# Seven products of sums of quarters (Strassen) for the second matrix of layer 0's MLP, in two of its eight chunks

## The chip, the core and the metric

The kernel runs on one core of a Trainium2 chip. The metric is the device time of one execution in microseconds (us); 2351.22 us is the median of 3 runs of the kernel before. Names of engines: PE is TensorE's matmul, PEld its weight load, DVE is VectorE, ACT is ScalarE, POOL is GpSimd, SP is SyncE, which issues the DMAs here.

## The reference, cut to what matters

The kernel computes two blocks of a network in float32. The second block has two layers over two streams of 256 tokens each, x and a context; each layer mixes tokens, normalises, and runs an MLP. The change touches the MLP of the second block's layer 0 alone, which both streams go through:

```python
def sq_relu_mlp(u, w1, b1, w2, b2):
    return jnp.square(jax.nn.relu(u @ w1 + b1)) @ w2 + b2

# in layer l, D_MODEL = 1024, hidden width 4096:
x = layer_norm(alpha * x + g2 * sq_relu_mlp(x * (1.0 + sc2) + sh2, w1[l], b1[l], w2[l], b2[l]), ln2_g[l], ln2_b[l])
if with_ctx:   # layer 0
    ctx = layer_norm(alpha * ctx + cg2 * sq_relu_mlp(ctx * (1.0 + csc2) + csh2, w1[l], ...), ln2_g[l], ln2_b[l])
```

## The kernel before, in words

**Precision.** PE multiplies in a format of fewer bits than float32, so every operand is split into a high part (an ACT cast) and a low part (a DVE subtraction of the high part from the original), and each product is three matmuls: high by high, high by low, low by high (`mm3`, L350 to L352). A weight tile of 128x1024 goes through `w()`: SP loads the raw tile `wr`, ACT casts it to `wh` (L343), DVE makes `wl` (L344). Raw, high and low tiles have four buffers each.

**The MLP of layer 0** (about 1415 to 1768 us of the trace) works on 512 tokens, four token tiles of 128: tiles 0 and 1 are the context, 2 and 3 are x. The 4096 hidden features are taken in eight chunks of 512, counted hc = 0 to 7. `up(hc)` multiplies four weight tiles of `w1` (eight k-tiles of 128 each) with the input `uh`, `ul`, which gives a chunk of hidden features; ACT makes relu and square and the high part `hh` (L431), DVE the low part `hl` (L432). `down(hc)` multiplies that chunk with four weight tiles of `w2`, for each half nn of the 1024 output features and each half kc of the chunk's features, over four token tiles: 96 matmuls of 512 columns. Results land in PSUM (tiles `mm`, six banks) and are added onto the accumulators `facc` in SBUF by DVE (L1677; chunk 0 is copied by ACT, L1675). In the loop up(hc+1) stands ahead of down(hc), so a pair of 96 + 96 matmuls repeats seven times; down(7) is left at the end.

**Side work.** Each `w()` ends with one step of a generator of other work. In chunks 1 to 4 this is the modulation of layer 1: `mr` tiles are loaded and multiplied onto `macd` by DVE (L892), four steps of 128x512 per loaded tile. After it come the residual rows. Each engine executes its instructions in one fixed order, in which the side work is interleaved.

**The end.** In chunks 6 and 7 `tail` multiplies the results by a gate row (`tl`, L1707) and adds them to the residual `resb` (L1710). In down(7) the token tiles 2 and 3 come first, then 0 and 1. When tiles 2 and 3 are done, their statistics run (BN_STATS L1037, BN_AGGR L1038, `brs`, `bmr` L1048), their scaling on DVE (L1054) and ACT (L1052), and then PE transposes them (L1015, tiles `tp`) into the input of layer 1. The transposes stand in PE's order behind 84 of down(7)'s 96 matmuls, and layer 1's first matmuls behind them. Layer 1's own MLP goes through the same function `mlp`.

## Time and profile before

| what | value |
|---|---|
| median of 3 runs | 2351.22 us (2349.1 to 2352.89) |
| the profiled execution's own time | 2352.55 us |
| its span | 2350.8 us |
| PE, PEld busy | 2278.8 us, 1967.8 us |
| DVE, ACT, POOL busy | 1712.0 us, 1117.2 us, 68.9 us |
| mean granted clock of TensorE | 0.989 |

All rows come from one profiled execution. The span is the time between its first and its last instruction. A busy time counts how long an engine had an instruction in work; instructions overlap in an engine's pipeline, so the distance between two starts can be shorter than the duration shown. Idle time on an engine that is not the bottleneck costs nothing by itself. The clock is in parts of full speed, 1.00 being 2.4 GHz and 0.50 being 1.2 GHz.

### The profile page before, as it was taken

How to read it: one execution, taken by the hardware profiler on the slowest of the kernel's cores; microseconds unless marked ns; L12 is line 12 of the kernel's file. 1: busy time of each engine (PE TensorE's matmuls, PEld its weight loads, DVE VectorE, ACT ScalarE, POOL GpSimd, SP SyncE). 2: the span in 40 equal slices, each digit the busy share in tenths (PEclk: the TensorE clock that was granted, in tenths of full speed). 3: DMA queues.
4: the chain of work that ended last, by engine and by line, in shares of the span. 5: the costliest groups of instructions: out<-in, count | busy, mean ns of one | idle time of the engine just before them, and what ended most of it. 6: DMA issues, size and time to landing. Idle time of an engine off the chain costs nothing.

```text
span 2350.8 us, 35308 instructions
## 1 busy us (share of the span) xinstructions
PE 2278.8 (97%) x13784; PEld 1967.8 (84%) x13796; DVE 1712.0 (73%) x2779; ACT 1117.2 (48%) x1702; POOL 68.9 (3%) x72
## 2 busy tenths in 40 slices
PE   8999989999999999999999999999999999998997
PEld 7989868889999888778777778888889898787996
DVE  6788878977766668985755777677568778776667
ACT  5655545554465444433453326434226543544653
POOL 1011100000000000000000000000000000000000
PEclk9999999999999999999999999999999999999999
DMA  5666546765555543223213735556324344345663
GB/s 199 217 188 191 186 138 225 256 217 191 187 179 186 187 154 111 68 72 94 94 47 106 238 95 179 168 174 197 120 90 150 118 136 127 97 138 180 203 190 115
DMA packets 124743, 364.73 MB, mean 155 GB/s; under 512 B 31840, under 2 KB 33632, under 8 KB 124576
## 3 DMA queue, kind: packets, MB, share of 16 engines
q1 hardware_dynamic: 124576, 362.47, 48.4%
q8 instruction: 108, 1.77, 0.3%
q14 instruction: 59, 0.48, 0.1%
HBM read 357.02 MB, written 3.31 MB: 153 GB/s over the span
## 4 chain that ended last, share of the span: by engine, by line
PE 52%; DVE 5%; issue 1%; ACT 1%; POOL 0%; DVEq 0%; POOLq 0%
PE mm L350 16%; PE mm L351 16%; PE mm L352 15%; PE mm L1437 1%; DVE cy L1149 1%; PE mm L1451 1%; DVE wl L344 1%; PE tp L718 1%; PE mm L1328 1%; PE tp L901 0%; PE tp L1015 0%; PE mm L1286 0%; DVE bst L1037 0%; DVE tl L1707 0%; DVE resb L1710 0%
## 5 line engine op out<-in xcount | busy, mean ns | idle before, releaser
L343 ACT CAST wh<-wr 128x1024 fp32r<-128x1024 f32 (+1 forms) x544 | 566.5, 1044 | 889.7 <-PE mm L351 475.5
L344 DVE TENSOR_TENSOR wl<-wr,wh 128x1024 fp32r<-128x1024 f32 (+1 forms) x544 | 659.3, 1214 | 333.6 <-ACT wh L343 324.8
L351 PE MATMUL mm<-ul,wh 128*128 128x256 f32 (+1 forms) x2224 | 704.5, 319 | 2.6 <-DVE ul L432 1.3
L352 PE MATMUL mm<-uh,wl 128*128 128x256 f32 (+1 forms) x2224 | 704.3, 319 | 2.7 <-DVE wl L344 2.7
L350 PE MATMUL mm<-uh,wh 128*128 128x256 f32 (+1 forms) x2224 | 699.9, 321 | 4.7 <-ACT m_q L1253 1.5
L350 PEld LDWEIGHTS mm<-uh,wh 128*128 128x128 f32 x2224 | 417.0, 190 | 43.1 <-ACT wh L343 5.0
L352 PEld LDWEIGHTS mm<-uh,wl 128*128 128x128 f32 x2224 | 422.3, 190 | 34.9 <-DVE wl L344 3.7
L351 PEld LDWEIGHTS mm<-ul,wh 128*128 128x128 f32 x2224 | 422.5, 190 | 33.9 <-issue 1.8
L351 PE MATMUL mm<-wl,hh 128*128 128x512 f32 x640 | 249.6, 391 | 0.0
L352 PE MATMUL mm<-wh,hl 128*128 128x512 f32 x640 | 249.2, 391 | 0.0
L350 PE MATMUL mm<-wh,hh 128*128 128x512 f32 x640 | 247.6, 391 | 0.0
L892 DVE SCALAR_TENSOR_TENSOR macd<-mr,silu_c,macd 128x512 f32<-128x512 f32 x336 | 238.3, 745 | 7.2 <-DMA mr<-in_w_mod 5.2
L350 PE MATMUL mm<-wh,uh 128*128 128x256 f32 x576 | 165.4, 291 | 2.7 <-ACT qk L575 1.5
L351 PE MATMUL mm<-wl,uh 128*128 128x256 f32 x576 | 163.5, 286 | 1.4 <-DVE wl L344 1.4
L352 PE MATMUL mm<-wh,ul 128*128 128x256 f32 x576 | 163.0, 285 | 0.1
L350 PEld LDWEIGHTS mm<-wh,hh 128*128 128x128 f32 x640 | 120.0, 188 | 28.1 <-issue 3.4
L352 PEld LDWEIGHTS mm<-wh,hl 128*128 128x128 f32 x640 | 120.1, 188 | 26.6 <-issue 0.8
L351 PEld LDWEIGHTS mm<-wl,hh 128*128 128x128 f32 x640 | 120.1, 188 | 26.5 <-DVE hl L432 0.8
L1149 DVE SCALAR_TENSOR_TENSOR cy<-hpad,vecl,cy 128x512 f32<-128x512 f32 (+1 forms) x240 | 136.8, 611 | 0.0
L350 PEld LDWEIGHTS mm<-wh,uh 128*128 128x128 f32 x576 | 108.5, 190 | 9.7 <-issue 4.6
L351 PEld LDWEIGHTS mm<-wl,uh 128*128 128x128 f32 x576 | 109.2, 190 | 3.4 <-DVE wl L344 2.1
L352 PEld LDWEIGHTS mm<-wh,ul 128*128 128x128 f32 x576 | 109.1, 190 | 0.7 <-DVE ul L465 0.3
(292 smaller groups left out, 2817.4 us busy)
## 6 DMA issues: line engine op xcount, KB each, us to landing
wr<-in_m SPq DMA_DIRECT2D x128, 512.0 KB
wr<-in_w SPq DMA_DIRECT2D x128, 512.0 KB
wr<-in_w_in SPq DMA_DIRECT2D x116, 512.0 KB
mr<-in_w_mod SPq DMA_DIRECT2D x96, 512.0 KB
wr<-in_a_wqkv SPq DMA_DIRECT2D x72, 512.0 KB
wr<-in_b_win SPq DMA_DIRECT2D x24, 512.0 KB
wr<-in_w_out SPq DMA_DIRECT2D x16, 512.0 KB
wr<-in_w_uq SPq DMA_DIRECT2D x16, 384.0 KB
```

Of the source, the lines that this page charges most:

```text
L343: self.last_hi = nc.scalar.copy(hi[:, :n], raw[:, :n]).ins
L344: self.last_lo = nc.vector.tensor_tensor(lo[:, :n], raw[:, :n], hi[:, :n].bitcast(F32), ALU.subtract).ins
L350: mm(out, lh, rh, start=first, stop=False)
L351: mm(out, lh, rl, start=False, stop=False)
L352: self.last_mm = mm(out, ll, rh, start=False, stop=last).ins
L718: nc.tensor.transpose(tp[:, b * P:b * P + P], pm[:, b * P:b * P + P], self.ident)
L892: nc.vector.scalar_tensor_tensor(out=a, in0=raw[:, k], scalar=sc, in1=a, op0=ALU.mult, op1=ALU.add)
L1149: nc.vector.scalar_tensor_tensor(out=ys[ft], in0=src, scalar=wk, in1=ys[ft], op0=ALU.mult, op1=ALU.add)
L1328: nc.tensor.matmul(pn[:, d * 130:d * 130 + 129], dts[d][:, s, i * P:i * P + P], v[:, s, 0:129], start=s == ks[0], stop=s == ks[-1])
L1437: nc.tensor.matmul(sc[:, 0:n * P], qs[hp * 2 + i][:, t * P:t * P + P], ks[:, hp * 2 + i, 0:n * P], start=True, stop=True)
L1451: nc.tensor.matmul(pos[hp][i * 64:i * 64 + 64, t * P:t * P + P], v[:, j, h * 64:h * 64 + 64], pt[i][:, j * P:j * P + P], start=j == 0, sto ...
```

## The change

Layer 0's MLP gets a function of its own, `mlp_wide`; layer 1 keeps `mlp`. In the chunks hc = 2 and hc = 4 (`SEVEN`) the product of the hidden chunk and its part of `w2` is taken in quarters: the hidden activations by token half (256 tokens) and feature half kc, the weights by kc and output half nn. Seven products (`PRODUCTS`, Strassen's scheme) take the place of eight. For each: a sum or difference of two activation quarters (`as`, DVE, in five of seven), its split into `ah` (ACT) and `al` (DVE), a sum or difference of two raw weight quarters (`bs`, DVE, 128x1024, in five of seven), its split in the buffers of `wh` and `wl`, 12 matmuls into two PSUM banks, and for each output quarter that it belongs to two adds or subtractions onto `facc` (24 in all per chunk, where there were eight). The steps of up(hc+1) and of the seven products alternate as `TURNS` says.

The other chunks keep their 96 matmuls, but split the hidden activations in four pieces of 128x512 at the start of the down step (`down_plain`, `down_last`), from a ring of four `ah` and four `al` buffers, in place of two pieces of 128x1024 right after up. `tail` for the sum of the first seven chunks is written after the loop (`result`) and no longer within chunk 6. The rows of the residual and the gates take turns in three buffers instead of five.

```diff
+PRODUCTS = (
+    (((0, 0),), None, ((0, 1), (1, 1)), ALU.subtract, ((0, 1, ALU.add), (1, 1, ALU.add))),
+    (((1, 0), (0, 0)), ALU.subtract, ((0, 0), (0, 1)), ALU.add, ((1, 1, ALU.add),)),
...
+    (((0, 1), (1, 1)), ALU.subtract, ((1, 0), (1, 1)), ALU.add, ((0, 0, ALU.add),)),
+)
+SEVEN = (2, 4)
+TURNS = (0, 0, 1, 1, 0, 1, 1, 0, 1, 1, 1)
...
+        def split_a(src):
+            ah = self.t(self.xm, [P, 2, half], "ah", F32R, bufs=4)
+            al = self.t(self.xm, [P, 2, half], "al", F32R, bufs=4)
+            self.split(ah, al, src)
+            return ah, al
+        def down(hc, rs):
...
+            def raw(kc, nn):
+                if (kc, nn) not in Bs:
+                    Bs[kc, nn] = t = self.t(self.xm, [P, 1024], "wq", bufs=3)
+                    self.last_w = nc.sync.dma_start(t, w2[nn, hc * 2 + kc].rearrange("p k f -> p (k f)")).ins
+                    self.spin(self.side_n)
+                return Bs[kc, nn]
+            for i, (qa, opa, qb, opb, outs) in enumerate(PRODUCTS):
+                y = quarter(rs, qa[0])
+                if opa is not None:
+                    y_ = self.t(self.xm, [P, 2, half], "as")
+                    nc.vector.tensor_tensor(y_, y, quarter(rs, qa[1]), opa)
+                    y = y_
+                ah, al = split_a(y)
+                ws = [raw(*q) for q in qb]
+                w = ws[0]
+                if opb is not None:
+                    w = self.t(self.xm, [P, 1024], "bs")
+                    nc.vector.tensor_tensor(w, ws[0], ws[1], opb)
+                bh = self.t(self.wp, [P, 1024], "wh", F32R, bufs=self.wbufs[1])
+                bl = self.t(self.wp, [P, 1024], "wl", F32R, bufs=self.wbufs[1])
+                self.last_hi = nc.scalar.copy(bh, w).ins
+                self.last_lo = nc.vector.tensor_tensor(bl, w, bh.bitcast(F32), ALU.subtract).ins
+                W = WT(bh, bl, 2, 512)
+                pts = [self.ps() for _ in range(nj)]
+                for j in range(nj):
+                    self.lin_t(pts[j], W, 0, 512, ah, al, j * P)
+                for j in range(nj):
+                    for T, nn, op in outs:
+                        a = acc(T * nj + j, nn)
+                        nc.vector.tensor_tensor(a, a, pts[j], op)
...
+        def down_plain(hc, rs):
+            hid = [[split_a(quarter(rs, (T, kc))) for T in range(2)] for kc in range(2)]
...
+        for hc in range(7):
+            u, d = up(hc + 1), down(hc, rs) if hc in SEVEN else None
+            for step in TURNS if d else (0,) * 4:
+                if step:
+                    next(d)
+                else:
+                    rs_ = next(u)
+            if d is None:
+                down_plain(hc, rs)
+            rs = rs_
+        for j in range(4):
+            for nn in range(2):
+                result(j, nn, acc(j, nn))
+        down_last(rs)
...
-            self.mlp(uh, ul, q0, 512, A[f"w1_{l}"], A[f"w2_{l}"], lambda f: self.vecl(f"b1_{l}", f), evac,
-                     self.by_quarters(self.make_u([0], aff, *u)) + [(0, KT, 0, 256)] if l == 0 else self.by_quarters(), MT[2], ready)
+            if l == 0:
+                self.mlp_wide(uh, ul, A["w1_0"], A["w2_0"], bias, accs, result,
+                              self.by_quarters(self.make_u([0], aff, *u)) + [(0, KT, 0, 256)], MT[2], ready)
```

The order of instructions on DVE where chunk 2's products end, in the changed kernel. `facc` rows are adds onto the accumulators, `bs` is a sum of two weights, `al` a low part of activations, `wl` a low part of a weight (`wl_15060` that of the seventh product, `wl_15085` of the next up), `macd` is side work:

```order
L873 TENSOR_TENSOR facc_2397_13767<-facc_2397_13767,mm_14997 128x512 x2
L861 TENSOR_TENSOR bs_15057<-wq_15019,wq_14783 128x1024
L873 TENSOR_TENSOR facc_2398_13768<-facc_2398_13768,mm_14998 128x512 x2
L449 TENSOR_TENSOR al_15250<-r_14687,ah_15249 128x512
L1036 SCALAR_TENSOR_TENSOR macd_14737<-mr_14954,silu_c_85,macd_14737 128x512 x2
L449 TENSOR_TENSOR al_15254<-r_14851,ah_15253 128x512
L873 TENSOR_TENSOR facc_2397_13767<-facc_2397_13767,mm_15033 128x512
L873 TENSOR_TENSOR facc_2399_13769<-facc_2399_13769,mm_15033 128x512
L873 TENSOR_TENSOR facc_2398_13768<-facc_2398_13768,mm_15034 128x512
L873 TENSOR_TENSOR facc_2400_13770<-facc_2400_13770,mm_15034 128x512
L865 TENSOR_TENSOR wl_15060<-bs_15057,wh_15059 128x1024
L361 TENSOR_TENSOR wl_15085<-wr_15082,wh_15084 128x1024
```

The same engine in the kernel before, at the adds that follow chunk 1's down step and the start of the pair with chunk 2, from one low part of a weight to the next ones:

```order
L344 TENSOR_TENSOR wl_15009<-wr_15006,wh_15008 128x1024
L892 SCALAR_TENSOR_TENSOR macd_14725<-mr_15012,silu_c_85,macd_14725 128x512 x2
L1677 TENSOR_TENSOR facc_2397_13767<-mm_14841,facc_2397_13767 128x512
L1677 TENSOR_TENSOR facc_2398_13768<-mm_14842,facc_2398_13768 128x512
L892 SCALAR_TENSOR_TENSOR macd_14725<-mr_15012,silu_c_85,macd_14725 128x512 x2
L1677 TENSOR_TENSOR facc_2399_13769<-mm_14843,facc_2399_13769 128x512
L1677 TENSOR_TENSOR facc_2400_13770<-mm_14844,facc_2400_13770 128x512
L344 TENSOR_TENSOR wl_15045<-wr_15042,wh_15044 128x1024
L1677 TENSOR_TENSOR facc_2397_13767<-mm_14921,facc_2397_13767 128x512
L344 TENSOR_TENSOR wl_15098<-wr_15095,wh_15097 128x1024
```

Between two low parts there stood at most four adds and four steps of side work; now there also stand the sum that the low part is made from, and pieces of activations for the chunk after.

PE at the same place of the changed kernel: `mm_15063` and `mm_15064` belong to the seventh product, `mm_15033` and `mm_15034` to the sixth, `mm_15080`, `mm_15081` and `mm_15167` to the up step that follows:

```order
L368 MATMUL mm_15034<-wl_15030,ah_15015 128x512
L369 MATMUL mm_15034<-wh_15029,al_15016 128x512
L367 MATMUL mm_15063<-wh_15059,ah_15053 128x512
L367 MATMUL mm_15064<-wh_15059,ah_15053 128x512
L367 MATMUL mm_15080<-uh_13388,wh_15084 128x512
L368 MATMUL mm_15080<-ul_13389,wh_15084 128x512
L367 MATMUL mm_15081<-uh_13388,wh_15120 128x512
L368 MATMUL mm_15081<-ul_13389,wh_15120 128x512
L367 MATMUL mm_15167<-uh_13388,wh_15171 128x512
L368 MATMUL mm_15167<-ul_13389,wh_15171 128x512
L368 MATMUL mm_15063<-wl_15060,ah_15053 128x512
L369 MATMUL mm_15063<-wh_15059,al_15054 128x512
```

Eight matmuls that use only high parts stand ahead of the first one that uses `wl_15060`.

DVE at the end of the stage in the changed kernel, up to the statistics (`bmr`) and the scaling of token tile 2 (`resb_2319`); `resb_2317` and `resb_2318` are the tiles of the context:

```order
L361 TENSOR_TENSOR wl_16772<-wr_16769,wh_16771 128x1024
L1182 BN_AGGR bmv_16559<-bst_16561 128x2
L1861 TENSOR_TENSOR resb_2317_13355<-resb_2317_13355,tl_16683 128x512
L1181 BN_STATS bst_16573<-resb_2320_13358 128x6
L1858 TENSOR_TENSOR tl_16686<-mm_16592,row_14241 128x512
L361 TENSOR_TENSOR wl_16785<-wr_16782,wh_16784 128x1024
L423 TENSOR_SCALAR brs_16560<-bmv_16559 128x1
L1181 BN_STATS bst_16697<-resb_2317_13355 128x6
L1182 BN_AGGR bmv_16571<-bst_16573 128x2
L1861 TENSOR_TENSOR resb_2318_13356<-resb_2318_13356,tl_16686 128x512
L1192 TENSOR_SCALAR bmr_16567<-bmv_16559,brs_16560 128x1
L1198 TENSOR_SCALAR resb_2319_13357<-resb_2319_13357,bmv_16559,brs_16560 128x512
```

The same place in the kernel before:

```order
L1710 TENSOR_TENSOR resb_2320_13358<-resb_2320_13358,tl_16364 128x512
L1038 BN_AGGR bmv_16379<-bst_16381 128x2
L1037 BN_STATS bst_16393<-resb_2320_13358 128x6
L406 TENSOR_SCALAR brs_16380<-bmv_16379 128x1
L1038 BN_AGGR bmv_16391<-bst_16393 128x2
L406 TENSOR_SCALAR brs_16392<-bmv_16391 128x1
L1048 TENSOR_SCALAR bmr_16387<-bmv_16379,brs_16380 128x1
L1054 TENSOR_SCALAR resb_2319_13357<-resb_2319_13357,bmv_16379,brs_16380 128x512
L344 TENSOR_TENSOR wl_16571<-wr_16568,wh_16570 128x1024
L1707 TENSOR_TENSOR tl_16495<-mm_16403,row_14237 128x512
L344 TENSOR_TENSOR wl_16584<-wr_16581,wh_16583 128x1024
```

The weights' low parts and the context's tail stood behind `bmr` and the scaling, and stand ahead of them now.

## Rows read from the trace of the kernel before

**Rows 1.** The page's first part: engine, busy us, share of the span, instructions.
```profile
span 2350.8 us, 35308 instructions
PE 2278.8 (97%) x13784; PEld 1967.8 (84%) x13796; DVE 1712.0 (73%) x2779; ACT 1117.2 (48%) x1702; POOL 68.9 (3%) x72
```

**Rows 2.** Busy time by stretch, pairs 2 to 5; columns as the first line.
```profile
core 0: us, PE busy (x) PEld busy (x) DVE busy (x) ACT busy (x) POOL busy (x), PEclk, DMA share, GB/s
...
1527.90:1572.10 44.20, 44.20 (x196) 36.61 (x195) 34.30 (x49) 16.90 (x19) 0.00 (x0) 1.00 0.63 195
1572.10:1616.30 44.20, 44.20 (x199) 35.66 (x198) 35.29 (x48) 17.01 (x21) 0.00 (x0) 1.00 0.60 184
1616.30:1660.50 44.20, 44.20 (x200) 35.66 (x199) 33.97 (x44) 17.33 (x20) 0.00 (x0) 1.00 0.59 178
1660.50:1704.80 44.30, 44.30 (x200) 35.76 (x199) 20.15 (x27) 14.99 (x16) 0.00 (x0) 1.00 0.32 100
```

**Rows 3.** Timeline of PE, start and duration: two matmuls, the second 24 later.
```profile
1531.11 0.39 PE L350 MATMUL mm<-uh,wh 128*128 128x512 f32 x1
...
1536.55 0.39 PE L350 MATMUL mm<-uh,wh 128*128 128x512 f32 x1
```

**Rows 4.** Groups, 1430 to 1740 us: count | busy us, mean ns | idle before, releaser.
```profile
L892 DVE SCALAR_TENSOR_TENSOR macd<-mr,silu_c,macd 128x512 f32<-128x512 f32 x112 | 78.0, 746 | 3.8 <-DMA mr<-in_w_mod 3.8
L344 DVE TENSOR_TENSOR wl<-wr,wh 128x1024 fp32r<-128x1024 f32 x57 | 69.7, 1223 | 71.8 <-ACT wh L343 71.5 <-PE mm L351 0.3
...
L1677 DVE TENSOR_TENSOR facc<-mm,facc 128x512 f32<-128x512 f32 x44 | 29.6, 686 | 8.8 <-PE mm L352 8.8
```

**Rows 5.** Timeline of DVE, start and duration, at two places.
```profile
1418.75 0.69 DVE L432 TENSOR_TENSOR ul<-mt,uh 128x512 fp32r<-128x512 f32 x1
1419.36 0.54 DVE L1022 TENSOR_SCALAR mt<-tp,aff_a,aff_b 128x256 f32<-128x256 f32 x1
...
1527.85 0.69 DVE L1677 TENSOR_TENSOR facc<-mm,facc 128x512 f32<-128x512 f32 x1
1528.45 0.75 DVE L892 SCALAR_TENSOR_TENSOR macd<-mr,silu_c,macd 128x512 f32<-128x512 f32 x1
1529.11 0.69 DVE L1677 TENSOR_TENSOR facc<-mm,facc 128x512 f32<-128x512 f32 x1
...
1530.53 1.22 DVE L344 TENSOR_TENSOR wl<-wr,wh 128x1024 fp32r<-128x1024 f32 x1
1531.66 1.41 DVE L892 SCALAR_TENSOR_TENSOR macd<-mr,silu_c,macd 128x512 f32<-128x512 f32 x2
```

**Rows 6.** Waits, 1439.4 to 1749: us in total, times, longest.
```profile
ACT wh L343 <- PE mm L351: 84.5, 28, 5.0
ACT wh L343 <- PE mm L352: 82.4, 23, 5.1
```

**Rows 7.** Timeline of DVE and PE, end of the stage; in brackets the idle before.
```profile
1734.54 1.22 DVE L344 TENSOR_TENSOR wl<-wr,wh 128x1024 fp32r<-128x1024 f32 x1
...
1763.45 0.21 DVE L1048 TENSOR_SCALAR bmr<-bmv,brs 128x1 f32<-128x1 f32 x1 [0.34 <-POOL brs L408]
...
1768.03 1.03 PE L1015 MATMUL tp<-cst,resb 128*128 128x128 f32 x8
...
1775.58 0.39 PE L351 MATMUL mm<-ul,wh 128*128 128x256 f32 x1 [1.33 <-DVE ul L432]
```

**Rows 8.** Waits of PE, 2150 to 2200: us in total, times, longest.
```profile
PE tp L1015 <- ACT resb L1052: 7.2, 1, 7.2
```

**Rows 9.** Busy time by stretches of 2 us behind that wait, columns as in rows 2.
```profile
2152.00:2154.00 2.00, 0.00 (x0) 0.00 (x0) 1.34 (x5) 1.46 (x2) 0.99 (x2) 0.55 0.99 315
2154.00:2156.00 2.00, 1.85 (x8) 1.57 (x8) 0.10 (x1) 0.66 (x2) 0.00 (x0) 0.50 0.97 293
2156.00:2158.00 2.00, 1.62 (x8) 1.37 (x8) 1.66 (x4) 1.69 (x3) 0.00 (x0) 0.50 1.03 416
2158.00:2160.00 2.00, 2.00 (x15) 2.00 (x14) 1.82 (x4) 1.69 (x4) 0.00 (x0) 0.75 1.03 389
```

More of the change, by code (lines that the diff above doesn't have):

```diff
@@ L759, in down @@
             if hc == 7 and bias is not None:
-                groups = [([0, 1], [j, j + 1]) for j in (2, 0)] if n == 512 else [([0, 1], [j]) for j in range(2)]
+                groups = [([0, 1], [j]) for j in range(2)]
             Ws = {}
@@ L788, in mlp, with mlp_wide, up, quarter @@
             hid = nxt
+    def mlp_wide(self, uh, ul, w1, w2, bias, accs, result, parts, mt, ready):
+        nc = self.nc
+        half, nj = 256, 2
+        first, n, c0, c1 = parts, 512, 0, 512
+        acc = lambda j, nn: accs[j][:, nn * 512:nn * 512 + 512]
+        def up(hc):
+            rs = []
+            pre = self.tiles([w1[f, 0] for f in range(4)], uh, ul, c0, c1, first) if hc == 0 else []
+            if hc == 0:
+                self.side_n = 1
+            for c in range(2):
+                r = self.t(self.xm, [P, 2, n], "r", bufs=4)
+                pv = pre[c * 2:c * 2 + 2] or [self.ps() for _ in range(2)]
+                for f in range(2):
+                    if hc:
+                        self.lin_f(pv[f], self.w(w1[hc * 4 + c * 2 + f, 0], 8, 128), 0, uh, ul, c0, c1)
+                    if f == 0:
+                        yield
+                for f in range(2):
+                    nc.scalar.activation(r[:, f, :], pv[f], AF.Relu, bias=bias(hc * 4 + c * 2 + f))
+                nc.scalar.activation(r, r, AF.Square)
+                rs.append(r)
+                self.tick(mt[min(hc, 1)])
+                yield rs
+        def quarter(rs, q):
+            return rs[q[1]][:, :, q[0] * half:q[0] * half + half]
+        def split_a(src):
[4 more added lines that the diff above has]
+        def down(hc, rs):
+            Bs = {}
+            def raw(kc, nn):
[28 more added lines that the diff above has]
+                        nc.vector.tensor_tensor(a, a, pts[j], op)
+                if i in (2, 6):
+                    self.tick(mt[min(hc, 1)])
+                yield
+        def down_plain(hc, rs):
+            hid = [[split_a(quarter(rs, (T, kc))) for T in range(2)] for kc in range(2)]
+            for nn in range(2):
+                pts = [self.ps() for _ in range(4)]
+                for kc in range(2):
+                    W = self.w(w2[nn, hc * 2 + kc], 2, 512)
+                    for j in range(4):
+                        self.lin_t(pts[j], W, 0, 512, *hid[kc][j // 2], j % 2 * P, first=kc == 0, last=kc == 1)
+                for j in range(4):
+                    a = acc(j, nn)
+                    if hc == 0:
+                        nc.scalar.copy(a, pts[j])
+                    else:
+                        nc.vector.tensor_tensor(a, a, pts[j], ALU.add)
+                self.tick(mt[1])
+        def down_last(rs):
+            Ws, nns = {}, [0, 1]
+            for js in ([2, 3], [0, 1]):
+                hid = [split_a(quarter(rs, (js[0] // 2, kc))) for kc in range(2)]
+                pts = {(nn, j): self.ps() for nn in nns for j in js}
+                for nn in nns:
+                    for kc in range(2):
+                        if (nn, kc) not in Ws:
+                            Ws[nn, kc] = self.w(w2[nn, 14 + kc], 2, 512)
+                        if nn == kc == 1 and js[0] == 0:
+                            self.turn(ux, 2)
+                        for j in js:
+                            with self.after_tp():
+                                self.lin_t(pts[nn, j], Ws[nn, kc], 0, 512, *hid[kc], j % 2 * P, first=kc == 0, last=kc == 1)
+                if js[0] == 0:
+                    self.turn(ux, 2)
+                for nn in nns:
+                    for j in js:
+                        result(j, nn, pts[nn, j])
+                ux = ready(js)
+                self.tick(mt[1])
+        for rs in up(0):
+            pass
+        for hc in range(7):
[3 more added lines that the diff above has]
+                    next(d)
+                else:
+                    rs_ = next(u)
+            if d is None:
+                down_plain(hc, rs)
+            rs = rs_
+        for j in range(4):
+            for nn in range(2):
+                result(j, nn, acc(j, nn))
+        down_last(rs)
@@ L969, in residual @@
         with self.pinned():
[L970 removed]
+            G.update({s: self.gate_row(l, 1, s, 3) for s in ss})
         yield
```

39 lines of the change are left out of this document (20 added, 19 removed).

## The prediction, made before the changed kernel was run

> **What bounds the kernel now.** I read the page's busy table first: TensorE (PE) is busy for 97% of the span, VectorE (DVE) for 73%, ScalarE (ACT) for 48% [rows 1]. Then I cut the changed stage, the MLP of layer 0, into its loop bodies. One body, a pair below, is up(p+1) followed by down(p), and takes 44.2 us. In pairs 2, 3 and 4 PE is busy in all of it, at full clock, and DVE for 34.3, 35.3 and 34.0 us; in pair 5, where the side work has run out, DVE has 20.2 [rows 2]. So PE sets the time here, by count: 24 matmuls of 512 columns start in 5.44 us, 0.2267 us each [rows 3]. The waits say the same from the other side: the ACT casts that make a weight's high part wait for PE to free a buffer (84.5 and 82.4 us in all), so the weights run ahead of PE as far as four buffers allow [rows 6]. To the reader this means two things: fewer matmuls shorten the stage, and DVE has about 10 us of slack in a pair that carries side work, no more.
>
> DVE's prices are start-to-start distances in a run without a wait, not durations. An add onto an accumulator lasts 0.69 and the next starts 0.60 after it; a modulation step (macd) 0.75 and 0.66; a weight's low part (128x1024) 1.22 and 1.13; a 128x512 split 0.69 and 0.61 [rows 5]; the groups' means confirm the durations over the stage [rows 4].
>
> **Part 1: fewer matmuls.** A Strassen chunk runs 7 products of 12 matmuls, 84 where there were 96. Two chunks save 24: 24 x 0.2267 = **-5.4 us**. All of it is on the path, PE being the bound.
>
> **Part 2: more DVE work in pairs 2 and 4.** Per Strassen chunk: 7 low parts and 5 sums of weights, 12 x 1.135 = 13.6; 5 sums of activations and 7 splits, 12 x 0.61 = 7.3; 24 adds onto accumulators, 24 x 0.60 = 14.4; together 35.3. Before it was 4 low parts 4.5, 8 adds 4.8 and 2 large splits 2.3, together 11.6. So +23.7 in a pair that shrinks by 12 x 0.2267 = 2.7 to 41.5. Pair 2 would need 34.3 + 23.7 = 58.0. Nor can it be spread: pairs 2 to 4 hold 103.6 of DVE now [rows 2], which becomes 151 in at most 3 x 44.2 = 132.6.
>
> How much of the excess PE feels depends on how far DVE can run ahead, so I count along DVE's new order in pair 2, with T0 the start of up(3). The split al_14818 takes a ring slot that a matmul 25 before T0 frees (T0-5.7); the cast and the split follow, 1.2 us: DVE is past it at T0-4.4. From there to the last product's low part wl_15060 (first order listing) stand 9 low parts and 4 weight sums, 14.8; 26 adds, 15.6; 20 macd steps, 13.2; 12 activation sums and splits, 7.3; small ones 0.9: 51.8 us. So wl_15060 is ready at T0+47.4 even if DVE never idles. PE has by then only 4 ups of 24 and 6 products of 12 to do, 168 x 0.2267 = 38.1. The gap is 9.3; PE's order (second listing) puts 8 matmuls there that need only a high part, 1.8. **Stall 7.5 us.** The macd steps could give way only if the order were another; it is fixed.
>
> Pair 4, counted alike from wl_15532, which is ready 1.2 us before its pair's start, to the last product's wl_15798: 12 large ones 13.6, 23 adds 13.8, 16 macd 10.6, 12 small splits and sums 7.3, 0.6: 45.9, hence +44.7; against PE 38.1 to 38.5, less 1.8: **stall 4.4 us**. Side work is less there, and DVE has caught up in pair 3, whose plain chunk needs what it did.
>
> Bounds: the trace shows no DVE sum of two raw weights, and no add with its operands exchanged. Nearest are the low part and the accumulator add [rows 5], and I take their start distances, which are of this very stage. At nine tenths of all these prices the two counts shrink by 5.2 and 4.6 and the stalls are 2.3 and 0 (rival B); if every instruction costs its full duration, each stall grows by 6 (rival D).
>
> Cover: the 1024-wide raw weights that wait in three buffers add no bytes, since each quarter is loaded once as before; DMA is at 0.56 to 0.63 of its share there [rows 2]. ACT gets 7 casts of each kind per chunk in place of 4 and 2, about 3 x 1.05 + 5 x 0.6, some 6 us on a base of 17 [rows 2]: hidden, but it stands between DVE's sum and DVE's low part, so it lengthens the chain rather than shortens it.
>
> **Part 3: the start.** A sum of two weights stands in DVE's order ahead of the last two low parts of the input: 0 to 2 us if its loads are late, covered by 47 matmuls that don't need them. I take **0.3**.
>
> **Part 4: plain chunks and the end.** Plain chunks split their hidden activations in four pieces within the down step: 4 x 0.61 for 2 x 1.135, nothing in pairs where DVE has slack (pair 5: 24 us). At the end it costs. Let E be the start of the last down: its 84th matmul ends at 1768.03 [rows 7], so E = 1749.0. Before, DVE reaches the statistics of tile 2 (bmr) at 1763.45 = E+14.4, the transposes start unstalled at E+19.0, and layer 1's stream runs from 1775.58 = E+26.6. After, the last four splits use a ring of four slots still held by the chunk before, and the tail's products of all tiles come in one block after the loop (third listing). From the low part at 1734.54 = E-14.5 [rows 7] to bmr: 7 low parts 7.9, 8 adds 4.8, 4 splits 2.4, 28 tail operations 16.8, 5 statistics 3.0, small 0.6, and 3.3 of waiting for slots: 38.8, so E+24.3. Scaling of tiles 2 and 3 follows on DVE and ACT, ready at E+26.5. PE has its 84 matmuls done at E+19.0 and idles 7.5. Then transposes and the 12 kept matmuls cover what was 1.9 of gaps before, and layer 1 begins near E+31.3: **+5 us** net (bounds: 0 if DVE needn't wait and the block is spread; 7.5 if none of the old gaps goes).
>
> **Part 5: the clock.** Late in the trace PE waits 7.2 us for ACT [rows 8]; the granted clock is 0.55 in the slice in which that ends, 0.50 in the next two and 0.75 in the fourth, so 1.85 + 1.62 + about 1.0 us of busy time ran at the lower level, 1.2 GHz, where it could have taken half [rows 9]: 2.2 us. Of the new idles the end's (7.5 us) is the one as long and unbroken as this; pair 2's has loose matmuls in it. **+2.2**, once.
>
> The Trainium skill ("TensorE: Matmul & The Clock Gate", HAM oscillation) says the gate falls wherever PE idles long enough between bursts; rows 9 agree for one such idle. By it pair 2's stall would pay as well, another 2.2, which is in rival D.
>
> **Sum.** -5.4 + 7.5 + 4.4 + 0.3 + 5.0 + 2.2 = +14.0. The profiled execution took 2352.55 us (span 2350.8), 1.3 above the median of 2351.22; so 2366.6 for such an execution and **2365** for a median. Against a saving of 5.4 stand four terms of which any two outweigh it.
>
> **Rivals.**
> A. PE's count decides. DVE's backlog is absorbed by the slack of 10 us a pair and by buffers filled in advance, and both stalls and the end vanish: 2351 - 5.4 = 2346. For it: PE waits for nothing in these pairs now [rows 2, 6]. Against: 51.8 us of DVE work between two fixed points 42.5 us apart [rows 5].
> B. The stalls about cancel the saving: 2350 to 2356. It needs DVE at nine tenths of its prices (stalls 2.3 and 0) and no fall of the clock: 2351 - 5.4 + 2.3 + 0.3 + 5.0 = 2353. For it: sums of two raw tiles are not in this trace, so their price is not known to a tenth; against: the other kinds, which are most of the count, run at the distances that I took [rows 5].
> C. The pairs stall as worked out and the end doesn't, or the other way round. Pairs alone: 2351 - 5.4 + 11.9 = 2357.5. End alone: 2351 - 5.4 + 7.2 = 2353, up to 2361 with half a pair's stall.
> D. DVE pays each instruction's full duration as soon as the kinds mix, and the clock falls at each stall: 71 instructions between the fixed points x 0.085 = 6.0 a chunk, 12 for both, and a second 2.2: 2365 + 10 to 14, so 2372 to 2379. For it: durations are 0.69, 0.75 and 1.22; against: the rows at 1527.85 to 1531.66 mix three kinds at the shorter distance [rows 5].
> E. The change doesn't do what it says: the products take as many matmuls, or the side work moves out of the pairs. The listings show neither, so I give it no chance of its own.
>
> The Trainium skill ("VectorE: DVE Perf Modes", The DRAIN you can't avoid) states that the next operation starts only when the pipeline is empty, and its rules for authors ask for few operations rather than for clever ones; that speaks against seven products. Rows 5 differ on the price: starts 0.60 apart where an operation lasts 0.69. By the rule D would be the forecast, 2372 to 2379; by the rows it is 2365.
>
> **How the numbers follow.** The forecast (2361 to 2370) has 0.42, C 0.24, D 0.13, B 0.12, A 0.09. Measurements of this kernel can tell about 0.2% (4.7 us) from no change. Faster by more than that is A: 0.09. Within it is B with a part of C's lower end: 0.16. Slower: 0.75. The range leaves out A and the upper half of D: **2350 to 2375**. The likeliest's own is 2361 to 2370.
>
> **What would show it.** PE's idle time in pair 2 just ahead of the first low-part matmul of the seventh product, near 7.5 us, with DVE busy without a break before it; one of about 4.4 in pair 4 and none in pairs 1, 3 and 5; the time from the first pair to the last down +6 (7.5 + 4.4 - 5.4); PE waiting near 7 us for the transposes at the end, with the granted clock under 1 behind it. I am wrong if DVE shows idle time in pairs 2 and 4 (then the chain through ACT or the loads decides), if the stall falls at an earlier product, or if the end is unstalled because DVE has its block done before E+19.

## The result, and the profile after

The changed kernel takes 2370.62 us (median of 6 runs, 2366.4 to 2372.95) where the kernel before takes 2350.16 in the same runs: a ratio of 1.0082, 95% interval 1.0069 to 1.0094, so **19 us slower** by the ratio. The prediction was 2365 us, 14 us slower, with a range of 2350 to 2375; the measured median lies in the range and 0.6 us above the part of it that was called likeliest (2361 to 2370).

The page's first part of the changed kernel, to be read against [rows 1]:

```profile
span 2370.1 us, 35407 instructions
PE 2287.0 (96%) x13772; PEld 1965.3 (83%) x13772; DVE 1758.8 (74%) x2859; ACT 1127.4 (48%) x1730; POOL 68.9 (3%) x72
```

DVE is busy for 46.8 us more, close to the 2 x 23.7 = 47.4 of the prediction. The span grows by 19.3. The starts of matmuls in the two timelines say where; the fourth column is the prediction's terms:

| stretch, by the first matmul of each | before | after | difference | predicted |
|---|---|---|---|---|
| pairs 2 and 3 (up(3) to up(5)) | 88.26 | 95.32 | +7.1 | -2.7 + 7.5 = +4.8 |
| pairs 4 and 5 (up(5) to up(7)) | 89.50 | 94.94 | +5.4 | -2.7 + 4.4 = +1.7 |
| end: down(6) to the long run of layer 1's matmuls | 61.51 | 68.61 | +7.1 | +5.0 + 2.2 = +7.2 |

The long run is what starts behind the last transposes of the stage, at 1788.74 before and 1807.47 after. The rest of the stage is unchanged. From up(0)'s last transposes to this long run it takes 360.9 us before and 380.5 after. I call this **the stage** below; it leaves out what varies ahead of it (its start lay between 1415 and 1428 us in the profiles of this case).

Pairs 2, 3 and 4 after, in the same view as [rows 2]:

```profile
1526.80:1571.00 44.20, 42.28 (x178) 32.20 (x176) 44.20 (x68) 20.33 (x26) 0.00 (x0) 1.00 0.47 142
1571.00:1615.20 44.20, 44.00 (x174) 33.61 (x175) 37.90 (x50) 16.31 (x20) 0.00 (x0) 0.93 0.66 198
1622.20:1666.40 44.20, 42.28 (x182) 32.20 (x180) 43.37 (x61) 21.00 (x27) 0.00 (x0) 1.00 0.35 102
```

The roles have changed: in pair 2 DVE is busy in all 44.2 us and PE is not; in pair 4 DVE for 43.4. Where PE waits stands in its timeline, at the end of the sixth product and the seventh:

```profile
1567.10 0.39 PE L369 MATMUL mm<-wh,al 128*128 128x512 f32 x1
1568.97 0.73 PE L367 MATMUL mm<-wh,ah 128*128 128x512 f32 x2 [1.48 <-ACT wh L864]
1569.92 0.50 PE L367 MATMUL mm<-uh,wh 128*128 128x512 f32 x1 [0.22 <-ACT wh L360]
...
1572.41 0.63 PE L368 MATMUL mm<-ul,wh 128*128 128x512 f32 x1
1573.24 0.79 PE L368 MATMUL mm<-wl,ah 128*128 128x512 f32 x1 [0.20 <-DVE wl L865]
1573.83 0.63 PE L369 MATMUL mm<-wh,al 128*128 128x512 f32 x1
1574.26 0.63 PE L367 MATMUL mm<-wh,ah 128*128 128x512 f32 x1
```

And DVE in the same microseconds:

```profile
1564.69 1.24 DVE L861 TENSOR_TENSOR bs<-wq,wq 128x1024 f32<-128x1024 f32 x1
1565.83 1.30 DVE L873 TENSOR_TENSOR facc<-facc,mm 128x512 f32<-128x512 f32 x2
...
1568.95 0.70 DVE L449 TENSOR_TENSOR al<-r,ah 128x512 fp32r<-128x512 f32 x1
1569.55 2.50 DVE L873 TENSOR_TENSOR facc<-facc,mm 128x512 f32<-128x512 f32 x4
1571.94 1.24 DVE L865 TENSOR_TENSOR wl<-bs,wh 128x1024 fp32r<-128x1024 f32 x1
1573.08 1.24 DVE L361 TENSOR_TENSOR wl<-wr,wh 128x1024 fp32r<-128x1024 f32 x1
```

PE has its sixth product done at 1567.3, then spreads eight matmuls that need only high parts over almost 6 us, and its first matmul with the seventh low part starts at 1573.24. Pair 2 began at 1526.84, so that is T0 + 46.4; the prediction had 47.4. DVE has no idle time there. The idle time of PE has to be taken over the distances of the starts, because loose matmuls stand in between: 1567.33 to 1573.24 is 5.9 us, less 1.8 for the eight matmuls leaves 4.1; in pair 4 it is 3.8 by the same count (1662.71 to 1668.35).

PE's waits in the two stalls name ACT first, and two rows of ACT say why:

```profile
PE mm L367 <- ACT wh L864: 3.0, 2, 1.5
PE mm L367 <- ACT wh L360: 0.9, 4, 0.2
PE mm L368 <- DVE wl L865: 0.2, 1, 0.2
```
```profile
1567.36 0.62 ACT L448 CAST ah<-r 128x512 fp32r<-128x512 f32 x1 [2.15 <-PE mm L368]
1567.88 1.04 ACT L864 CAST wh<-bs 128x1024 fp32r<-128x1024 f32 x1
```

This is a second hold-up at the same place. The cast of the seventh product's weight (L864) stands in ACT's order behind the cast of a piece of the next chunk's activations (L448), and that one waits for a slot of the ring of four `ah` buffers until PE has ended the sixth product. The sum `bs` had been ready since 1565.93. The casts that follow on ACT feed the loose matmuls. By this path alone PE could have begun the low parts at about 1572.84 (the last loose matmul's start plus 0.43), and it began at 1573.24; in pair 4 at about 1668.30, and it began at 1668.35. So the two paths end nearly together in the changed kernel. Which of them sets the time is told by the run with the column sums together, below.

The granted clock behind it (columns as in [rows 2], stretches of 2 us):

```profile
1568.00:1570.00 2.00, 0.81 (x3) 0.38 (x3) 2.00 (x4) 2.00 (x3) 0.00 (x0) 1.00 0.94 371
1570.00:1572.00 2.00, 1.78 (x5) 0.91 (x6) 2.00 (x5) 1.76 (x2) 0.00 (x0) 0.67 0.82 285
1572.00:1574.00 2.00, 1.80 (x5) 0.98 (x5) 2.00 (x3) 0.00 (x0) 0.00 (x0) 0.50 0.05 14
1574.00:1576.00 2.00, 2.00 (x7) 1.52 (x6) 2.00 (x3) 0.00 (x0) 0.00 (x0) 0.50 0.25 57
1576.00:1578.00 2.00, 2.00 (x7) 1.63 (x6) 2.00 (x4) 0.52 (x1) 0.00 (x0) 0.62 0.77 272
```

The clock fell to 1.2 GHz in this stall too, though PE ran loose matmuls in it: matmuls start 0.43 apart up to 1577, ten of them, some 2 us lost. It was at 0.67 and 0.50 already while the loose matmuls ran.

At the end, PE's wait, the statistics on DVE, PE's transposes, and the clock:

```profile
PE tp L1159 <- ACT resb L1196: 7.1, 2, 6.4
```
```profile
1785.10 0.21 DVE L1192 TENSOR_SCALAR bmr<-bmv,brs 128x1 f32<-128x1 f32 x1
```
```profile
1779.44 0.39 PE L369 MATMUL mm<-wh,al 128*128 128x512 f32 x1
1786.20 0.69 PE L1159 MATMUL tp<-cst,resb 128*128 128x128 f32 x2 [6.38 <-ACT resb L1196]
```
```profile
1786.00:1788.00 2.00, 1.03 (x4) 0.64 (x5) 1.09 (x3) 0.96 (x2) 0.51 (x1) 0.50 0.31 123
1788.00:1790.00 2.00, 2.00 (x9) 1.81 (x8) 0.71 (x2) 1.33 (x3) 0.00 (x0) 0.50 0.00 0
1790.00:1792.00 2.00, 2.00 (x7) 1.52 (x6) 1.92 (x4) 1.01 (x2) 0.00 (x0) 0.50 0.04 8
```

The last down starts 96 x 0.2267 behind 1738.86, at E = 1760.6; bmr comes at E+24.5 (predicted 24.3; before 14.4, [rows 7]), the transposes start 6.5 us late, and PE runs at the lower clock for about 6 us.

One thing in the timeline was not in the prediction: the four column sums over `macd` (into `tp`) stand together in before and apart after. Before, and then after:

```profile
1576.76 1.06 PE L901 MATMUL tp<-macd,cst 128*32 128x512 f32 x8
```
```profile
1554.13 1.04 PE L1045 MATMUL tp<-macd,cst 128*32 128x512 f32 x2
1561.00 1.05 PE L1045 MATMUL tp<-macd,cst 128*32 128x512 f32 x2
1591.76 1.05 PE L1045 MATMUL tp<-macd,cst 128*32 128x512 f32 x2
1593.40 1.05 PE L1045 MATMUL tp<-macd,cst 128*32 128x512 f32 x2
```

Each sum fills a quarter of the columns of the array and shows as two records. Eight records take 1.0 us, two records alone also take 1.0 (the next matmul starts 0.98 behind), so the set costs 3.9 in place of 1.0. Two of these four pieces lie in pair 2, ahead of the stall.

### The profile page after: what moved, and what is told of

Its sections match the earlier page's. It is cut to its first block, busy times and chain, and to the rows that moved or that the text cites. A ratio compares the mean times of both kernels' runs of the same rounds, so it can differ in the third digit from the quotient of the medians.

```text
span 2370.1 us, 35407 instructions
## 1 busy us (share of the span) xinstructions
PE 2287.0 (96%) x13772; PEld 1965.3 (83%) x13772; DVE 1758.8 (74%) x2859; ACT 1127.4 (48%) x1730; POOL 68.9 (3%) x72
## 4 chain that ended last, share of the span: by engine, by line
PE 51%; DVE 6%; issue 1%; ACT 1%; POOL 0%; DVEq 0%; POOLq 0%; ACTq 0%
PE mm L367 15%; PE mm L368 15%; PE mm L369 15%; PE mm L1581 1%; DVE cy L1293 1%; PE mm L1595 1%; DVE wl L361 1%; PE tp L735 1%; PE mm L1472 1%; PE tp L1045 1%; DVE macd L1036 1%; DVE facc L873 1%; PE tp L1159 0%; ACT wh L360 0%; DVE wl L865 0%
## 5 line engine op out<-in xcount | busy, mean ns | idle before, releaser
L360 ACT CAST wh<-wr 128x1024 fp32r<-128x1024 f32 (+1 forms) x536 | 557.3, 1043 | 811.1 <-PE mm L368 456.2
L361 DVE TENSOR_TENSOR wl<-wr,wh 128x1024 fp32r<-128x1024 f32 (+1 forms) x536 | 649.7, 1215 | 309.4 <-ACT wh L360 304.3
L368 PE MATMUL mm<-wl,hh 128*128 128x512 f32 x384 | 150.1, 392 | 0.0
L369 PE MATMUL mm<-wh,hl 128*128 128x512 f32 x384 | 149.7, 392 | 0.0
L367 PE MATMUL mm<-wh,hh 128*128 128x512 f32 x384 | 148.0, 393 | 0.0
L367 PE MATMUL mm<-wh,ah 128*128 128x512 f32 x248 | 97.6, 398 | 3.0 <-ACT wh L864 3.0
L368 PE MATMUL mm<-wl,ah 128*128 128x512 f32 x248 | 98.7, 399 | 0.2 <-DVE wl L865 0.2
L369 PE MATMUL mm<-wh,al 128*128 128x512 f32 x248 | 98.0, 396 | 0.0
```

The costliest lines, as they stand in the source:

```text
L360: self.last_hi = nc.scalar.copy(hi[:, :n], raw[:, :n]).ins
L361: self.last_lo = nc.vector.tensor_tensor(lo[:, :n], raw[:, :n], hi[:, :n].bitcast(F32), ALU.subtract).ins
L367: mm(out, lh, rh, start=first, stop=False)
L368: mm(out, lh, rl, start=False, stop=False)
L369: self.last_mm = mm(out, ll, rh, start=False, stop=last).ins
```

## The experiments

Two questions were open: whether DVE's throughput makes the stalls, or the chain from weight sum over ACT's cast to low part; and whether the end's delay belongs to the Strassen chunks at all. All ratios are to the kernel before on the same chip.

### The end

**No Strassen chunk** in the new function:

```diff
-SEVEN = (2, 4)
+SEVEN = ()
```

> The changed kernel with no Strassen chunk: all eight chunks take 96 matmuls, in the new function with its four-piece splits, its ring of four and its tail written after the loop. In the trace of the changed kernel PE came to the transposes of token tiles 2 and 3 6.5 us late (1786.2 for 1779.7) with the clock at half behind it. Theory (the end is a cost of its own, made by splits and tail): no stall in pairs 2 and 4, the transposes still start 5 to 7 us behind their 84 matmuls, and the time is 7 to 9 us above before, 2357 to 2359. Rival (the end is late because DVE carries a backlog out of the Strassen chunks): the transposes start on time and the time is that of before within 2 us, 2348 to 2352.

Measured: 2356.46 us, ratio 1.0021 (1.0012 to 1.0030), +5 us; the stage 368.2 us, +7.3. The median lies a little under the range that was written down, the stage in it. PE's only wait in the stage, and two idle times on DVE ahead of it:

```profile
PE tp L1159 <- ACT resb L1196: 7.1, 2, 6.4
```
```profile
1737.77 0.69 DVE L449 TENSOR_TENSOR al<-r,ah 128x512 fp32r<-128x512 f32 x1 [0.84 <-ACT ah L448]
1740.55 0.69 DVE L449 TENSOR_TENSOR al<-r,ah 128x512 fp32r<-128x512 f32 x1 [2.08 <-ACT ah L448]
```

The transposes start 6.54 us late, to 0.01 us as in the changed kernel. So the end is a cost of the rewritten function, not of Strassen: DVE waits 2.9 us for ACT's casts, which wait for slots of the ring, and does the rest late.

**Tail inside chunk 6**, still without a Strassen chunk:

```diff
                         nc.vector.tensor_tensor(a, a, pts[j], ALU.add)
+                    if hc == 6:
+                        result(j, nn, a)
...
-        for j in range(4):
-            for nn in range(2):
-                result(j, nn, acc(j, nn))
```

> The kernel with no Strassen chunk, with the tail of the first seven chunks' sum written inside chunk 6's down step as in before, and not after the loop; the ring of four slots for the last splits stays. DVE's order then has 13 and 12 tail operations and 4 low parts of weights between the eight last adds and the statistics of tile 2 (bmr), where the kernel with no Strassen chunk has 14, 14 and 6, and before 12, 12 and 3; the four small splits stand there still. Theory (each operation ahead of bmr counts): 5 fewer operations, 2 x 1.13 + 3 x 0.6 = 4.1 us earlier; PE's idle ahead of the transposes goes from 6.5 to about 2.5 us, the clock stays up, and the time falls by 4 to 6 us. Rival (the ring alone, by the 3 us in which DVE waits for a slot, holds up the end): the idle stays above 5 us and the time within 2 us of the kernel with no Strassen chunk.

Measured: 2353.27 us, ratio 1.0011 (1.0002 to 1.0020), by the ratios 2.4 us less than without this edit where 4 to 6 were written down; the stage 364.5, 3.7 less. The first transposes are on time, the next ones wait:

```profile
PE tp L1158 <- ACT resb L1195: 4.6, 3, 2.7
```

The longest idle is 2.7, where 2.5 was expected.

**A ring of its own** for the last four splits on top of that:

```diff
-        def split_a(src):
+        def split_a(src, tag=""):
...
-                hid = [split_a(quarter(rs, (js[0] // 2, kc))) for kc in range(2)]
+                hid = [split_a(quarter(rs, (js[0] // 2, kc)), "7") for kc in range(2)]
```

> The same with a ring of its own for the last chunk's four splits, so that they need not wait for chunk 6; DVE's order up to bmr has before's counts (12, 12, 3 and no split). Theory: no idle of PE ahead of the transposes, the time is that of before within 2 us. Rival (something else of the new function costs, the rows' three buffers or the four-piece splits): 3 us or more above before.

Measured: 2350.91 us, ratio 1.0006 (0.9995 to 1.0016); no wait at the transposes; the stage 362.0, 1.1 above before. Both parts of the end are found: tail order and ring, about 3.7 and 2.4 us of the stage. The 1.1 that is left lies behind the first transposes, which come as early as in before; its cause stays open.

**Both Strassen chunks, only the end mended.** The last splits are made right after up(7), in the buffers `wq` and `bs`, and the tail inside chunk 6:

```diff
+                    if hc == 6:
+                        result(j, nn, a)
...
+            if hc == 6:
+                hids = split_last(rs_)
...
-        down_last(rs)
+        down_last(hids)
```

> The changed kernel with both Strassen chunks as they are and only its end mended: the tail inside chunk 6, the last four splits made right after up in buffers that the Strassen chunks have left. Theory (the end costs by itself, 5 us by the times and 7.5 by the trace of the kernel with no Strassen chunk): PE has no idle ahead of the transposes and the time is 5 to 7.5 us below the changed kernel, 2363 to 2366, the two stalls staying as they are. Rival (end and stalls are one backlog, of which a part shows wherever DVE is looked for): the idle moves to another place and the time stays within 2 us of 2370.6.

Measured: 2363.57 us, ratio 1.0054 (1.0040 to 1.0068), 6.6 us under the changed kernel by the ratios; the stage 373.9. Down(6) to layer 1's long run is 61.53, before 61.51. Pairs 2 and 3 take 95.6, 4 and 5 take 95.1, as in the changed kernel. End and stalls add up; they are not one backlog.

### The stalls

**Strassen in hc = 2 alone.**

```diff
-SEVEN = (2, 4)
+SEVEN = (2,)
```

> The changed kernel with Strassen in hc = 2 alone. By the trace of the changed kernel pairs 2 and 3 together cost 7.1 us net (95.3 for 88.3), pairs 4 and 5 5.4 net. Theory (the two chunks' stalls are separate, each made by its own pair's DVE load): the end's 5 to 7.5 plus 7.1, about 2362 to 2366, with the stall ahead of the seventh product unchanged, and pairs 4 and 5 as in before. Rival (the second chunk's stall comes from what the first left over): most of the loss of pair 4 stays in some form, 2367 or more, or pair 2's stall has another size.

Measured: 2364.53 us, ratio 1.0059 (1.0046 to 1.0071). Pairs 2 and 3 take 95.34 (95.32 in the changed kernel), 4 and 5 take 89.50 as before. The two stalls are separate.

**Fewer adds.** Ten of 24 adds per chunk are left out:

```diff
-                    for T, nn, op in outs:
+                    for T, nn, op in outs[:1]:
```

> The changed kernel without the second adds: each product is added onto the first of its output quarters only, so 10 of 24 adds per Strassen chunk are left out and the result of these chunks is incomplete. Matmuls, sums of weights, casts and loads stay. Theory (DVE's throughput sets the stall): DVE has 10 x 0.60 = 6.0 us less in pairs 2 and 4, so PE's idle ahead of the seventh product's low part shrinks from about 6.5 and 5.5 us to under 1, the clock doesn't fall there, and the time drops by 11 to 14 us, to about 2357 to 2360. Rival (the chain of weight sum, cast and low part, or the loads, sets it): the stall stays within 1.5 us of its size and the time within 4 us of 2370.

Measured: 2360.91 us, ratio 1.0040 (1.0026 to 1.0054), 9.9 us under the changed kernel by the ratios; a little less than was written down. PE waits for nothing in pairs 2 to 5, and DVE has idle time again, if little; pairs 2 and 4:

```profile
1525.50:1569.70 44.20, 44.20 (x190) 34.70 (x189) 43.75 (x64) 20.98 (x27) 0.00 (x0) 1.00 0.49 153
1614.60:1658.80 44.20, 44.20 (x188) 33.79 (x188) 41.38 (x56) 21.52 (x27) 0.00 (x0) 1.00 0.34 95
```

All sums, casts, low parts and loads are still there; with 6 us less on DVE there is no stall, and the clock stays at 1.00. But the order on ACT has changed too: the seventh product's weight is cast with one piece of the next chunk's activations ahead of it in pair 2 and none in pair 4, where there were two. So this run alone doesn't tell DVE's load from the wait for the ring. What is missing to the expected time are the column sums: pairs 2 and 3 take 89.1 and pairs 4 and 5 91.6, together 8.4 above before less 24 matmuls, and seven pieces too many stand in them, 0.98 each; 1.5 us of the 8.4 stay without a cause.

**Strassen where no side work runs**, hc = 5 alone:

```diff
-SEVEN = (2, 4)
+SEVEN = (5,)
```

> The changed kernel with its one Strassen chunk in hc = 5, whose pair carries no modulation steps. Theory (DVE's throughput): DVE needs 35.3 + 4.5 us and little side work in a pair of 41.5, so the seventh product comes without a stall over 1 us; the time is that of the kernel with no Strassen chunk less 12 matmuls, 2.7 us (about 2355). Rival (the chain through one buffer for weight sums and one for activation sums stalls by itself): a stall of 4 us or more ahead of the seventh product in pair 5 too, and 2 to 5 us more than the kernel with no Strassen chunk. A third outcome: the backlog is carried to the end and the transposes start later than in the kernel without Strassen chunks.

Measured: 2353.96 us, ratio 1.0011 (1.0003 to 1.0020), 2.5 us under the kernel with no Strassen chunk. Pairs 4 and 5 take 86.8 where before has 89.5: exactly the twelve matmuls. Pair 5:

```profile
1655.80:1700.00 44.20, 44.20 (x199) 35.68 (x198) 39.82 (x57) 21.68 (x27) 0.00 (x0) 1.00 0.17 49
```

DVE works 39.8 us, under the 41.5 of PE's matmuls, and PE waits for nothing. The scheme gains what its count says when DVE has room. Here, too, ACT's order has no piece of activations just ahead of the seventh product's weight.

**The column sums kept together**, in the three sections that the change had taken apart; the sum that is ready last is issued first:

```diff
+                t0 = None
+                order = ((1, 1), (1, 0), (0, 1), (0, 0)) if (l == 1 and sec >= 3) else ((0, 0), (0, 1), (1, 0), (1, 1))
+                for half, v in order:
+                    q = (half * 2 + v) * 32
+                    with self.tc.issue_after(t0) if t0 and (l == 1 and sec >= 3) else nullcontext():
+                        mi = nc.tensor.matmul(tp[q:q + 32, :], self.cst("ones")[:, 0:32], acc[:, half, v], start=True, stop=True, tile_position=(0, q)).ins
+                    t0 = t0 or mi
                 for half in range(2):
-                    for v in range(2):
-                        q = (half * 2 + v) * 32
-                        nc.tensor.matmul(tp[q:q + 32, :], self.cst("ones")[:, 0:32], acc[:, half, v], start=True, stop=True, tile_position=(0, q))
```

> The changed kernel with the four column sums over macd (the matmuls into tp, L1045) of three sections kept together in PE's order: in the changed kernel's trace two records of them alone take 0.98 us, and eight together took 1.00 in before, and they stand apart in pairs 2 to 5 (2+2+2+2, then 6+2, 4+2+2). Theory (apart they cost 1 us a piece on PE, a term that the prediction left out): those that stand ahead of a stall were hidden by it, the others were not, so the time drops by 2 to 4 us. Rival (they are all hidden by PE's stalls): no change within 1 us.

Measured: 2370.28 us, ratio 1.0081 (1.0068 to 1.0094): no change, the rival's outcome. PE is earlier at the seventh product and waits longer for it: the first matmul with its low part starts at T0 + 46.4 in both kernels. In pair 4 it even comes 0.85 later, and more matmuls run at the lower clock. This is also the answer on ACT: with PE at its sixth product's end 2.4 us earlier, the seventh product's weight is cast by T0 + 40.2, where it was 42.1, and nothing comes of it. DVE's order sets the low part. PE time saved ahead of a stall that DVE sets is worth nothing, and what would have shown behind it went back into stall and clock.

**The sums of weights on POOL.**

```diff
-                    nc.vector.tensor_tensor(w, ws[0], ws[1], opb)
+                    nc.gpsimd.tensor_tensor(w, ws[0], ws[1], opb)
```

> The changed kernel with the five sums of two weight quarters per Strassen chunk on POOL in place of DVE; POOL is busy for 3% of the span. What such a sum takes there no trace of this case shows. Theory (DVE's throughput): DVE has 5 x 1.135 = 5.7 us less in pairs 2 and 4, so if POOL makes a sum in under 5 us the stalls go as with fewer adds, from 6.5 and 5.5 to under 1.5 us, and the time falls by 8 to 11 us, to 2360 to 2363. Rival (the chain from sum to cast to low part is what PE waits for, or POOL and DVE slow each other): stalls of the same size or larger, at earlier products, DVE's durations above 0.70 for a 128x512 add, and a time of 2370 or more.

Measured: 2373.67 us, ratio 1.0103 (1.0089 to 1.0116), 5 us above the changed kernel by the ratios, whose intervals just touch; no gain in any case. POOL and DVE at the first such sum, in order of start:

```profile
1520.12 2.84 POOL L861 TENSOR_TENSOR bs<-wq,wq 128x1024 f32<-128x1024 f32 x1 [91.57 <-DVE wl L865]
1520.62 0.68 DVE L892 TENSOR_TENSOR facc<-facc,mm 128x512 f32<-128x512 f32 x1
1521.22 2.29 DVE L1036 SCALAR_TENSOR_TENSOR macd<-mr,silu_c,macd 128x512 f32<-128x512 f32 x1
1523.44 0.67 DVE L892 TENSOR_TENSOR facc<-facc,mm 128x512 f32<-128x512 f32 x1
```

POOL holds 1520.12 to 1522.96. The accumulator add, which reads one operand from PSUM, takes its usual 0.68 in the middle of it. The macd step, both operands in SBUF, takes 2.29 in place of 0.75 and ends half a microsecond behind POOL. So at this sum DVE loses about 1.5 us to save 1.135, and the sum comes later. Pairs 2 and 3 take 94.5, 0.8 less than in the changed kernel, pairs 4 and 5 take 98.5, 3.6 more. It is the rival's outcome by the second of its causes, though not on the adds that it named: those read PSUM.

### Versions that are faster

**The kernel before with its column sums together**, the same edit in all twelve sections.

> The kernel before, with the four column sums over macd kept together in PE's order in all twelve sections (the last one to become ready is issued first, the other three behind it). In before, five of the earlier sections have them apart (in 3, 3, 4, 3 and 2 pieces where 1 would do: 11 pieces too many), and apart a piece takes 0.98 us in the trace, four together 1.00. Theory (a piece costs PE about 1 us wherever PE is the bound): 5 to 10 us faster. Rival (in those stages PE waits for something else, or holding back the sums delays who needs them): within 2 us of before.

Measured: 2344.98 us, ratio 0.9975 (0.9966 to 0.9985): 6 us faster. (The pieces too many are 3 + 3 + 4 + 3 + 2 less 5, ten and not eleven; at 0.98 each they would be 9.8 us.)

**One Strassen chunk, hc = 5**, with the end mended and the sums together.

> One Strassen chunk, hc = 5, where no side work runs; the tail inside chunk 6 and the last four splits made right after up, in buffers that the Strassen chunk has left, so DVE's order at the end is that of before; the column sums kept together in all sections. Theory: 12 matmuls fewer, 2.7 us, with no stall and no late end, on top of what the sums together give in the kernel before: 2 to 4 us below that kernel. Rival (the chunk's 23.7 us of DVE work reach the end as a backlog): no better than that kernel.

Measured: 2344.38 us, ratio 0.9968 (0.9957 to 0.9979). The stage is 359.3, 1.6 under before: the pairs gained 2.7, and the end gave back 1.1, as in the run with the end restored. That is under what was written down, and by the runs' times it can't be told from the version without Strassen.

**Both chunks, side work moved.** As the last, with hc = 2 and 4:

```diff
+            self.side_n = 0 if d else 1
             for step in TURNS if d else (0,) * 4:
...
             if d is None:
+                self.side_n = 2 if hc in (1, 5) else 1
                 down_plain(hc, rs)
```

> Both Strassen chunks as in the change (hc = 2 and 4), with the mended end and the column sums kept together in all sections, and the side work moved: no modulation step is issued in pairs 2 and 4, two for each weight of the down steps of pairs 1 and 5, one elsewhere. DVE then has 35.3 + 4.5 us in a Strassen pair of 41.5. Theory (DVE's throughput alone made the stalls): pairs 2 and 4 have under 1 us of idle PE each, both chunks' 24 matmuls are gained (5.4 us), on top of the sums together (6 us): 2338 to 2341, faster than the kernel with one Strassen chunk by 2 to 4 us. Rival (the steps crowded into pairs 1 and 5 make a backlog that stalls pair 2 or the end): a stall of 3 us or more there and 2343 or more.

Measured: 2341.32 us, ratio 0.9966 (0.9952 to 0.9979), 0.3 us above what was written down. All of PE's waits in the stage:

```profile
PE mm L368 <- DVE ul L449: 1.8, 1, 1.8
PE tp L1178 <- DVE mt L1185: 0.9, 2, 0.5
```

Both lie at the end. Pairs 2 and 3 take 85.55, which is 88.26 less twelve matmuls to 0.01 us; the stage is 356.2, 4.7 under before. The same two Strassen chunks that cost 12.5 us gain 5.4 in their pairs once the side work beside them is gone. In time it is the fastest kernel here by median, 0.3% under before; the 2 to 4 us that it was to be ahead of the version with one chunk stand in the stages (356.2 and 359.3) and not in the ratios, and against both other mended versions the intervals overlap.

## Why the prediction was right, and where it was off

**Sign and mechanism** held. DVE became the bound in the two pairs, and the stall came at the product that was named; in pair 2 DVE is busy without a break before it, in pair 4 it has 0.8 us of idle time. It is throughput: PE and ACT came 2 us earlier in the run with the sums together, and the low part did not. The three runs with less DVE work beside the products (fewer adds, hc = 5, side work moved) have no stall; but ACT's order has changed in them as well, so how long a stall the wait for the ring alone would leave stays open. The prediction had ACT as hidden, with the remark that it lengthens the chain; that ACT would wait there for the ring was not in it. The total was forecast 5 us too low by the ratio, through the terms below.

**Matmuls saved, -5.4:** right; the version without stalls shows 2.7 a chunk.

**Pair 2, 7.5:** the low part was due at T0 + 47.4 and the matmul that needs it started at T0 + 46.4, 6.5 us late by the prediction's count of PE. As idle time only 4.1 of it shows, because PE itself came 2.4 later than counted, 2.0 of that by two pieces of column sums. From DVE's first start behind the split that waits for the ring slot (1521.40, or T0 - 5.4) to the low part's end (1573.18) it is 51.8 us, the count to 0.1; the count began 1.0 too late. The start-to-start prices were right; at the durations of rival D it would have been 53. DVE's rows after still show 0.70 for a split whose successor starts 0.60 later (1568.95). The Trainium skill ("VectorE: DVE Perf Modes", The DRAIN you can't avoid) itself says that an operation that isn't held starts earlier, and points to its section on two Vector instructions with no wait between them; the prediction's reading of it left this out.

**Pair 4, 4.4:** T1 + 46.2 where 44.7 was forecast (T1 = 1622.16, the matmul at 1668.35). Against PE's count of 38.1 and 1.8 that is 6.3 us late; 1.0 of it is a set of column sums that before has there too, so 5.3. Of the 1.5 that it came later, 0.8 is idle time on DVE, which the count took as none; the rest stays open.

**The clock, +2.2 once:** this step failed. The prediction kept it for the end because pair 2's stall has loose matmuls in it; the granted clock fell in that stall too, and in pair 4's for a shorter time, about 2.0 and 0.7 us. The half of rival D that spoke of the clock came true, the half that spoke of prices did not. The Trainium skill ("TensorE: Matmul & The Clock Gate", A second HAM failure mode: psum-queue depth-cycling) tells of a kernel whose PE idles briefly again and again between groups of matmuls, and whose clock goes to and fro between its two levels. The trace agrees as far as one stall can: the granted clock was 0.67 and 0.50 in pair 2's, between 1.00 before and 0.62 at its end.

**Column sums:** a term that was left out. Apart they add 1.0 us in pair 3 and 2.0 in pair 5 of the changed kernel's trace. With 6.5 + 2.0 + 1.0 and 5.3 + 0.7 + 2.0 the pairs' losses of 9.8 and 8.2 (differences above plus 2.7) are accounted for to 0.3. But the run with the sums together shows that this sum is not a list of independent prices: taking that term away gave nothing, since stall and clock took it over.

**The end, +5.0 and +2.2:** 7.1 measured for 7.2, with bmr at E+24.5 for 24.3. The cause was put right too: 3.7 us for the tail and 2.4 for the ring in the runs that undo them one by one. The transposes came 6.5 us late where 7.5 was counted.

**The start, +0.3:** nothing shows there.

**Two slips:** rival D's terms, 2365 + 10 to 14, give 2375 to 2379 and not 2372; and the share of DMA in pairs 2 to 4 is 0.59 to 0.63 by [rows 2].

## What to carry to other kernels

A scheme that trades matmuls for vector adds is paid by the engine that does the adds: count that engine's whole work between two fixed points of its order, side work too, before counting the matmuls saved. Here the same chunk cost 6 us beside side work and gained 2.7 without it. And when a loop is rewritten around a new idea, run the rewrite without the idea: a third of this loss was in the rewrite.

## What the runs showed of the hardware

- **Four narrow matmuls into different column quarters cost what one costs, as long as they stand together**: eight records 1.0 us, two alone 0.98. Where each is issued when its operand is ready, this is lost; keeping them together gave 6 us in the kernel before.
- **POOL held up some of DVE's work.** A DVE instruction with both operands in SBUF took 2.29 us in place of 0.75 beside a POOL sum, and ended when POOL had; one with a PSUM operand was not touched. The Trainium skill ("SBUF — State Buffer", Who interferes with whom) says that a DVE instruction with two SBUF inputs contends with a GpSimd instruction that reads SBUF, and that one with at most one SBUF input, outside its 2-port modes, doesn't. The trace agrees. POOL's sum of 128x1024 took 2.4 to 3.5 us.
- **The clock fell in a stall that holds matmuls**: in pair 2's, PE ran eight loose matmuls between 1568.97 and 1573.24, and the granted clock was 0.50 at its end.
